# Another job beside the second pair's gates, and two casts on other engines, in the recurrent branch of a hybrid encoder

## The chip, the cores and the metric

The kernel runs on one core of a Trainium2 chip. The metric is device time in microseconds (us) of one execution. The engines work side by side, each through its own queue in a fixed order: TensorE (PE, matmuls), VectorE (DVE), ScalarE (ACT), GpSimd (POOL), and the SP queue, which issues all DMAs here. Matmuls write PSUM; DVE and ACT read PSUM and SBUF; the GpSimd work here is all in SBUF.

## The reference, cut to what matters

Two residual layers (1024 tokens, width 1024). The even layer projects its normed input once and feeds two branches, differential attention and a bidirectional gated linear recurrence (RG-LRU); the odd layer is a neighbourhood attention. The recurrent branch is what the change touches:

```python
xc = lax.conv_general_dilated(x, conv_w[:, None, :], ...) + conv_b      # depthwise, width 4
za = einsum('bsnc,rncd->rbsnd', xb, w_a) + b_a                         # r: two directions
zx = einsum('bsnc,rncd->rbsnd', xb, w_x) + b_x
gate_a, gate_x = sigmoid(za), sigmoid(zx)
log_a = -LRU_C * gate_a * softplus(-lam)
u = sqrt(-expm1(2.0 * log_a)) * gate_x * xc
h = forward scan of (a[0], u[0]) + backward scan of (a[1], u[1])
...
mixed = concatenate([a_out * silu(g_a), b_out * silu(g_b)])            # then @ w_out
```

The recurrence has 512 channels, which the kernel holds as four chunks of 128 partitions by 1024 tokens.

## The kernel before, in words

Matrix products are made from split operands: a high part (a cast to a reduced 32-bit type, `fp32r`) and a low part (the rest after subtraction), three matmuls per product (`mm3`, lines 201 to 203): high by high, high by low, low by high. So every activation or weight that enters a matmul needs a cast for its high part and a subtraction for its low part. For weights, `split_next` does it (L185 on ACT, `whi`; L186 on GpSimd, `wlo`), slab by slab in the order of `order0`, one slab per 128 output columns.

`proj` computes 128 output channels for one half of the tokens (512) with 24 matmuls and hands the PSUM bank to an evacuation. Four banks go around in the recurrent branch, two each of two kinds (`bank`); a bank is free again when its evacuation has read it.

The jobs of the branch, in program order (lines 851 to 855):

- `xb(c)`: projects chunk c of the recurrent input; evacuated by an ACT copy (L418).
- `cv(c)`, `conv(c)`: the convolution. For chunks 2 and 3 GpSimd makes the first tap (L705), DVE adds three (L710). Then comes the high part `xch` (L715 on ACT for chunks 0 and 1, L717 on DVE for 2 and 3) and the low part `xcl` in two halves (L720, on DVE for chunks 0 and 1, on GpSimd for 2 and 3).
- `pair((c, c+1))`: for two chunks, sixteen gate products of three matmuls (name `gate`), each with a sigmoid on ACT (L751), a tanh per direction (L757) and a product on DVE (L759); after the sixteen, for each direction an exponential (L766), squares (L770) with a DVE step (L771), square roots (L777), products (L780), scans (L783, L785) and their sum (L787). In between `gate_w` splits the gate weights of a later chunk (L730 on ACT, `gwh`; L731 on GpSimd, `gwl`).
- `vj(h)`: head h's values for the attention; evacuated by an ACT copy (L425).
- `gb(c)`: the branch's own gate path for chunk c. Each half is evacuated by a tanh on ACT (L667), a DVE step that reads PSUM for the last time (L668), a product with the scans' result (L795, DVE), a high part (L799, ACT), a low part (L800, DVE), both in a strided order, and two DMAs that store them (L802).
- `kq0` and one half of the next keys: what the attention starts with.

`weave` interleaves jobs by hand, so many steps of each in turn. The framework then fixes the order of each engine's instructions ahead of the run: it walks the program with its own estimates of when each instruction's inputs are there, and gives a free engine what is ready, by program order, evacuations and weight splits first (`high_priority`). On the chip each engine keeps that order, whatever is really ready.

## Time and profile before

| | us |
|---|---|
| runs | 1191.19, 1193.62, 1196.17 |
| median | 1193.62 |
| the profiled execution, own time | 1190.94 |
| its span | 1189.2 |
| granted TensorE clock, mean | 0.994 |

The span is from the first to the last instruction of the profiled execution. The recurrent branch with the jobs named above takes about 60 to 231 us of it; the attention's first logits follow at 230.75. In a timeline row the first number is the start and the second the length, both in us from the span's start; rows of several instructions are marked x2, x3. Brackets hold the idle time of the engine just before the row and what ended it.

### The profile page before, as it was taken

To read this page: it belongs to the slowest core of one execution; us is meant where nothing else is said; L and a number is where in the kernel's file an instruction comes from. 1 tells how busy PE (TensorE), PEld (TensorE's weight loads), DVE (VectorE), ACT (ScalarE), POOL (GpSimd) and SP (SyncE) were. 2 spreads that over 40 slices of the span, in tenths; PEclk is the share of its full clock that TensorE was granted. 3 is DMA by queue.
4 is the path that set the end of the run, shared out by engine and by line. 5 is a ranking of instruction groups with operands and counts; after the bars stand their busy time and mean duration, and the time that the engine had idled before them with its cause. 6 is when DMAs were issued, how large, how long until landed. Compare 5 with 4: busy or idle time off the path is not lost.

```text
span 1189.2 us, 19214 instructions
## 1 busy us (share of the span) xinstructions
PE 1142.0 (96%) x7232; PEld 972.3 (82%) x7232; DVE 735.6 (62%) x1422; ACT 564.4 (47%) x1029; POOL 372.5 (31%) x346
## 2 busy tenths in 40 slices
PE   4999899999998999999999999999999999999997
PEld 3788668888887888777878888988998998888896
DVE  6867948699889989768763334233434443556354
ACT  4358486465655556523443444344444434445121
POOL 2124321243333322344413333332333333326100
PEclk8999999999999999999999999999999999999999
DMA  9723132422123112476513442243453544314212
GB/s 331 234 87 117 53 96 74 141 74 82 37 79 88 32 39 72 136 245 225 181 53 121 136 116 83 87 141 101 131 171 96 152 133 120 90 38 161 92 72 71
DMA packets 85789, 136.46 MB, mean 115 GB/s; under 512 B 8000, under 2 KB 49472, under 8 KB 85696
## 3 DMA queue, kind: packets, MB, share of 16 engines
q1 hardware_dynamic: 85696, 135.23, 36.4%
q8 instruction: 57, 0.93, 0.3%
q14 instruction: 36, 0.29, 0.1%
HBM read 112.13 MB, written 16.78 MB: 108 GB/s over the span
## 4 chain that ended last, share of the span: by engine, by line
PE 75%; DVE 12%; ACT 5%; DMA 3%; issue 2%; POOL 2%; SPq 0%; DVEq 0%; ACTq 0%; POOLq 0%
PE pp L201 14%; PE pp L203 14%; PE pp L202 14%; PE no L1383 4%; PE etr L1365 3%; PE v L201 2%; PE v L203 2%; PE v L202 2%; PE n L662 2%; PE atr L998 2%; DVE e L968 2%; PE n L663 2%; PE s L662 1%; PE s L663 1%; POOL wlo L186 1%
## 5 line engine op out<-in xcount | busy, mean ns | idle before, releaser
L201 PE MATMUL pp<-ahi,whi 128*128 128x512 f32 (+1 forms) x976 | 370.2, 379 | 1.0 <-DVE sgb L668 0.9
L203 PE MATMUL pp<-ahi,wlo 128*128 128x512 f32 (+1 forms) x976 | 367.7, 377 | 1.1 <-POOL wlo L186 1.1
L202 PE MATMUL pp<-alo,whi 128*128 128x512 f32 (+1 forms) x976 | 368.0, 377 | 0.0
L186 POOL TENSOR_TENSOR wlo<-raw,whi 128x1024 fp32r<-128x1024 f32 x80 | 196.8, 2463 | 267.6 <-ACT whi L185 249.1
L203 PEld LDWEIGHTS pp<-ahi,wlo 128*128 128x128 f32 x976 | 183.8, 188 | 35.4 <-POOL wlo L186 1.6
L201 PEld LDWEIGHTS pp<-ahi,whi 128*128 128x128 f32 x976 | 183.8, 188 | 34.0 <-DVE sgb L668 1.7
L202 PEld LDWEIGHTS pp<-alo,whi 128*128 128x128 f32 x976 | 183.9, 188 | 30.4
L1354 POOL TENSOR_SCALAR e<-e,r 128x288 f32<-128x288 f32 (+1 forms) x128 | 71.5, 572 | 234.7 <-DVE r L1352 234.4
L185 ACT ACTIVATE whi<-raw 128x1024 fp32r<-128x1024 f32 x80 | 84.3, 1056 | 105.3 <-PE pp L202 57.4
L972 ACT ACTIVATE e<-e,nm 128x1024 f32<-128x1024 f32 x64 | 73.6, 1150 | 47.1 <-DVE nm L968 46.7
L1349 ACT ACTIVATE e<-e,nm 128x288 f32<-128x288 f32 (+1 forms) x128 | 72.7, 569 | 46.1 <-DVE nm L1346 39.3
L1371 DVE COPY e<-etr 96x384 f32<-96x384 f32 (+1 forms) x64 | 35.5, 555 | 94.3 <-PE etr L1365 92.7
L1346 DVE CUSTOM_DVE_ANT_0 e<-n,bias 128x288 f32<-128x288 f32 (+1 forms) x128 | 60.6, 505 | 46.9 <-PE n L663 32.9
L1369 ACT ACTIVATE e<-etr 96x384 f32<-96x384 f32 (+1 forms) x64 | 31.3, 490 | 118.2 <-DVE e L1371 116.7
L968 DVE CUSTOM_DVE_ANT_0 e<-s,tb 128x1024 f32<-128x1024 f32 x64 | 77.3, 1219 | 6.7 <-PE s L663 4.9
L989 POOL TENSOR_SCALAR e<-e,r 128x256 f32<-128x256 f32 x32 | 32.7, 1021 | 131.6 <-DVE r L978 81.4
L201 PE MATMUL v<-whi,ahi 128*128 128x256 f32 x256 | 72.2, 282 | 0.0
L203 PE MATMUL v<-whi,alo 128*128 128x256 f32 x256 | 71.9, 281 | 0.0
L202 PE MATMUL v<-wlo,ahi 128*128 128x256 f32 x256 | 71.9, 281 | 0.0
L1005 ACT ACTIVATE ath<-atr 128x512 fp32r<-128x512 f32 x64 | 37.5, 596 | 38.1 <-PE atr L998 37.8
L1365 PE MATMUL etr<-ident,e 128*96 128x128 f32 (+1 forms) x384 | 52.5, 272 | 2.0 <-POOL e L1354 2.0
L662 PE MATMUL s<-ks,qq 128*128 128x512 f32 x128 | 52.5, 410 | 0.4 <-DVE nm L968 0.4
(218 smaller groups left out, 2108.5 us busy)
## 6 DMA issues: line engine op xcount, KB each, us to landing
raw<-in_w_dram SPq DMA_DIRECT2D x56, 512.0 KB
ada<-in_adaw_dram SPq DMA_DIRECT2D x96, 256.0 KB
raw<-in_wo_dram SPq DMA_DIRECT2D x24, 512.0 KB
bias<-in_nab_dram SPq DMA_DIRECT2D x64, 144.0 KB
qq<-qq SPq DMA_DIRECT2D x48, 128.0 KB
bias<-in_nab_dram SPq DMA_DIRECT2D x32, 192.0 KB
xT<-in_xT_dram SPq DMA_DIRECT2D x16, 256.0 KB
vd<-vt SPq DMA_DIRECT2D x32, 128.0 KB
```

The costliest lines, as they stand in the source:

```text
L185: A.activation(hi[:], raw[:], AF.Copy)
L186: G.tensor_tensor(lo[:], raw[:], hi[:], ALU.subtract)
L201: T.matmul(ps, lh, rh, start=start, stop=False)
L202: T.matmul(ps, lh, rl, start=False, stop=False)
L203: state["pe"] = T.matmul(ps, ll, rh, start=False, stop=stop).ins
L662: T.matmul(dst, qsel(q[m]), k, start=True, stop=False)
L968: state["dve"] = V.tensor_tensor_reduce(out=e[:], in0=ps[:].rearrange("p a b -> p (a b)"), in1=tbt["tb"][:, o:o + S], scale=-1.0, scalar=3 ...
L972: A.activation(e[:], e[:], AF.Exp, scale=-1.0, bias=nm[:], accum_out=sums[:, m:m + 1])
L1346: state["dve"] = V.tensor_tensor_reduce(out=e[:, m, :n], in0=ps[:, m, :n], in1=bias["now"][m][:, :n], scale=-1.0, scalar=3.0e38, op0=ALU.a ...
L1349: A.activation(e[:, m, :n], e[:, m, :n], AF.Exp, scale=-1.0, bias=nm[:, m:m + 1], accum_out=sums[:, m:m + 1])
L1354: state["pool"] = G.tensor_scalar(e[:, m, :n], e[:, m, :n], r[:, m:m + 1], 0.0, ALU.mult, ALU.add).ins
L1365: T.transpose(pt[:kn, m, j * P:(j + 1) * P], e[:, m, j * kn:(j + 1) * kn], ident[:])
```

## The change

Three things:

1. `vj(3)` and `gb(1)` change places. The second pair's gates are woven with `vj(3)` (one step of it to two gates, as before with `gb(1)`), and `gb(1)` comes right after, ahead of `gb(2)`. The weight slabs change places with them.
2. The high part of the convolution is made on ACT for all four chunks; L717 on DVE goes.
3. For chunk 0 alone, `gb`'s high part (L799) is made by GpSimd.

```diff
-    order0 = [c_xb, c_xb + 1, c_v, c_xb + 2, c_xb + 3, c_v + 1, c_v + 2, c_gb, c_gb + 1]
-    order0 += [c_v + 3, c_gb + 2, c_gb + 3, c_k, c_q]
+    order0 = [c_xb, c_xb + 1, c_v, c_xb + 2, c_xb + 3, c_v + 1, c_v + 2, c_gb, c_v + 3]
+    order0 += [c_gb + 1, c_gb + 2, c_gb + 3, c_k, c_q]
...
             xl = [kqp.tile([P, HF], F32R, tag=t, name=f"xcl{c}", bufs=3) for t in ("qq1", "qlo")]
-            if c < 2:
-                A.activation(xh[:], xc[:], AF.Copy)
-            else:
-                V.tensor_copy(xh[:], xc[:])
+            A.activation(xh[:], xc[:], AF.Copy)
...
                 hi, lo = t[:].bitcast(F32R), lo[:].bitcast(F32R)
-                A.activation(as_fours(hi), by_fours(m), AF.Copy)
+                if c:
+                    A.activation(as_fours(hi), by_fours(m), AF.Copy)
+                else:
+
+                    G.tensor_copy(as_fours(hi), by_fours(m))
                 V.tensor_tensor(as_fours(lo), by_fours(m), as_fours(hi), ALU.subtract)
...
                 cv(2), cv(3), vj(1), vj(2), mod_step(), gb(0), mod_step(),
-                weave(gb(1), pair((2, 3)), turns=(1, 2)),
-                vj(3), gb(2), gb(3), kq0(), proj(at0[c_k + 1], 0, evac_k(("a", 1)))]
+                weave(vj(3), pair((2, 3)), turns=(1, 2)),
+                gb(1), gb(2), gb(3), kq0(), proj(at0[c_k + 1], 0, evac_k(("a", 1)))]
```

## The prediction

> **What bounds the kernel now.** I read the page first, then the windows of this branch, then what TensorE (PE) waits for, and last each engine's timeline around those waits.

> ```profile
> span 1189.2 us, 19214 instructions
> PE 1142.0 (96%) x7232; PEld 972.3 (82%) x7232; DVE 735.6 (62%) x1422; ACT 564.4 (47%) x1029; POOL 372.5 (31%) x346
> ```

> PE is busy for 96% of the span and its matmuls stay the same in number and shape. Only its idle time can go. The recurrent branch has this much of it, by the windows (stretch, its length, PE busy) and by the waits from 60 to 235 us (total, times, longest):

> ```profile
> 140.00:174.00 34.00, 27.43 (x113) 20.36 (x112) 20.33 (x21) 24.67 (x32) 13.24 (x11) 1.00 0.21 72
> ...
> 187.00:205.00 18.00, 18.00 (x81) 14.93 (x80) 17.06 (x11) 8.91 (x9) 2.68 (x1) 1.00 0.17 56
> ```

> ```profile
> PE gate L201 <- DVE sgb L668: 3.9, 2, 2.1
> PE gate L201 <- ACT t L751: 1.7, 1, 1.7
> PE pp L201 <- DVE sgb L668: 0.9, 1, 0.9
> PE gate L203 <- POOL gwl L731: 0.7, 1, 0.7
> PE gate L201 <- ACT gwh L730: 0.3, 1, 0.3
> ```

> From 140 to 174 us PE idles 34.00 - 27.43 = 6.57 us, which the waits explain (3.9 + 1.7 + 0.7 + 0.3 = 6.6). With the 0.9 later, 7.5 us is all the change can win here, 0.6% of the time. A difference of 0.5% (6.0 us) is about what a measurement of this kernel can tell from none. In 187 to 205 us PE is full while VectorE (DVE) is busy for 17.06 of 18: a chain on DVE runs just inside PE's cover there.

> The three large waits, on PE, then ScalarE (ACT), DVE and GpSimd (POOL); brackets hold the idle time before a row and its releaser:

> ```profile
> 143.35 0.50 PE L201 MATMUL gate<-xch,gwh 128*128 128x512 f32 x1 [1.85 <-DVE sgb L668]
> ...
> 147.77 0.50 PE L201 MATMUL gate<-xch,gwh 128*128 128x512 f32 x1 [2.05 <-DVE sgb L668]
> ...
> 151.31 0.50 PE L201 MATMUL gate<-xch,gwh 128*128 128x512 f32 x1 [1.66 <-ACT t L751]
> ```

> ```profile
> 133.56 0.60 ACT L667 ACTIVATE sgb<-pp 128x512 f32<-128x512 f32 x1 [3.28 <-PE pp L203]
> 144.42 1.15 ACT L799 ACTIVATE sgb<-t 128x512 fp32r<-128x512 f32 x1 [10.26 <-DVE t L795]
> ...
> 146.42 0.58 ACT L667 ACTIVATE sgb<-pp 128x512 f32<-128x512 f32 x1
> ...
> 148.31 1.27 ACT L751 ACTIVATE t<-gate,sm 128x512 f32<-128x512 f32 x2
> 149.60 1.08 ACT L799 ACTIVATE sgb<-t 128x512 fp32r<-128x512 f32 x1
> 150.58 0.67 ACT L751 ACTIVATE t<-gate,sm 128x512 f32<-128x512 f32 x1
> ```

> ```profile
> 140.91 0.66 DVE L717 CAST xch<-xc 128x1024 fp32r<-128x1024 f32 x1
> ...
> 142.63 0.67 DVE L668 SCALAR_TENSOR_TENSOR sgb<-sgb,pp 128x512 f32<-128x512 f32 x1
> 143.34 1.05 DVE L795 SCALAR_TENSOR_TENSOR t<-t,sgb 128x512 f32<-128x512 f32 x1
> 145.60 1.06 DVE L800 TENSOR_TENSOR ylo<-t,sgb 128x512 fp32r<-128x512 f32 x1 [1.22 <-ACT sgb L799]
> ...
> 147.03 0.69 DVE L668 SCALAR_TENSOR_TENSOR sgb<-sgb,pp 128x512 f32<-128x512 f32 x1 [0.23 <-ACT sgb L667]
> ```

> ```profile
> 141.70 3.85 POOL L720 TENSOR_TENSOR xcl<-xc,xch 128x512 fp32r<-128x512 f32 x2 [9.65 <-issue]
> ```

> PE's gates need PSUM banks. Two are held by gb(0)'s halves until L668. The first L668 comes at 142.63, behind the first pair's scans and the cast at 140.91. The second comes at 147.03: its tanh (146.42) is queued on ACT behind the high-part cast L799, which sat 10.26 us waiting for DVE. The third wait is for a sigmoid (150.58) behind the second L799 (149.60). So ACT's in-order wait feeds two of the three.

> **The change part by part.**

> *GpSimd takes gb(0)'s high part.* Two L799 leave ACT, and its 10.26 us wait with them: the second tanh and the sigmoids come soon after their matmuls. The third wait goes (-1.6 of 1.66; its sigmoid still takes 0.67). The second half's L668 stays in the queue behind the first half's L800, which now waits for GpSimd. The trace has no one-input GpSimd copy with these strides; the nearest row is the scaling

> ```profile
> L1354 POOL TENSOR_SCALAR e<-e,r 128x384 f32<-128x384 f32 x64 | 37.9, 605 | 148.3 <-DVE r L1352 147.9 <-PE n L663 0.3
> ```

> By size that is 605 x 512/384 = 0.8 us at the low end. The high end is one L720, 3.85/2 = 1.9 us. L800, a strided pass on DVE, takes 1.06 against 0.67 for L668, so I scale 0.8 by that to 1.25 us. That is no faster than L799's 1.15. [...] The second wait so keeps most of its length, 1.5 of 2.05, if the copy gets ahead of the second L720, and 1.9 more, 3.4, if it queues behind both. I take 1.5 (-0.55).

> *The convolutions' casts go to ACT.* For chunk 3, DVE's 0.66 at 140.91 leaves the queue ahead of L668, worth up to 0.66 on the first wait; ACT was idle there (the 10.26), so its cast costs nothing. I take -0.4, since GpSimd's L720 starts earlier and can hold up DVE. For chunk 2 it is another matter:

> ```profile
> 103.48 2.59 DVE L710 SCALAR_TENSOR_TENSOR xc<-xb,sm,xc 128x1023 f32<-128x1023 f32 x2
> 106.18 0.70 DVE L717 CAST xch<-xc 128x1024 fp32r<-128x1024 f32 x1
> 106.79 3.47 DVE L759 TENSOR_TENSOR t<-t,xc 128x1024 f32<-128x1024 f32 x2
> ```

> ```profile
> 101.44 0.69 ACT L751 ACTIVATE t<-gate,sm 128x512 f32<-128x512 f32 x1 [0.31 <-PE gate L203]
> ...
> 103.58 0.58 ACT L418 ACTIVATE xb<-pp 128x512 f32<-128x512 f32 x1
> 104.06 1.84 ACT L751 ACTIVATE t<-gate,sm 128x512 f32<-128x512 f32 x3
> ```

> ```profile
> 104.64 0.39 PE L201 MATMUL gate<-xch,gwh 128*128 128x512 f32 x1
> ```

> ```profile
> L715 ACT ACTIVATE xch<-xc x2: 1060/1061/1062, 74.1 to 78.7; 128x1024 fp32r<-128x1024 f32 x2
> ```

> L759 for chunk 1 was ready when the twelfth of the pair's sixteen sigmoids ended (101.44 + 0.69 = 102.13), and is written earlier in the program, yet DVE has the convolution and its cast ahead of it. So the plan that fixes each engine's order holds conv(2) for done before 102.13; on the chip it ends at 103.48 + 2.59 = 106.07. A cast on ACT would be placed by that same plan next to the twelfth sigmoid, ahead of the copy at 103.58 and the sigmoids at 104.06. ACT then waits until 106.07, casts for 1.06 (its other 128x1024 casts, the last row) until 107.13, makes the next weight's high part (a cast of that shape, 1.0), and copies xb (0.58) from 108.1 to 108.7. The bank of that copy is what the sixteenth gate at 104.64 writes next, by the order in which banks are handed out. PE stops from 104.64 to about 108.7: +4.05. If the cast lands ahead of the twelfth sigmoid it is +5.25; if it slips into a gap after its data, 0 to +0.4. I take 4.05. ACT's chain behind it moves as far as PE does, so the later waits keep their size. GpSimd's L720 for chunk 2 starts at 107.1, about as now, so the weights queued behind it are not later.

> *vj(3) is woven with the second pair.* vj(3) has the same 48 matmuls, and its evacuations are ACT copies of 0.58 alone. The gb(1) steps leave the weave:

> ```profile
> 157.82 1.13 ACT L799 ACTIVATE sgb<-t 128x512 fp32r<-128x512 f32 x1
> 158.83 0.64 ACT L730 ACTIVATE gwh<-gwr 128x512 fp32r<-128x512 f32 x1
> ```

> The last chunk's gate weights came 1.13 late behind that L799; the waits on gwh and gwl, 0.3 + 0.7, go (-1.0, bounds 0 and -1.0). Its four DMA stores on the SP queue move later with gb(1); the weight loads on that queue go by slab order, and two equal-sized slabs change places: 0.

> *gb(1) covers the second pair's tail.* Here is the bill:

> ```profile
> 187.76 1.23 DVE L780 TENSOR_TENSOR t<-t,w 128x1024 f32<-128x1024 f32 x1 [1.68 <-ACT w L777]
> 189.02 2.29 DVE L783 TENSOR_TENSOR_SCAN t<-t,t 128x1024 f32<-128x1024 f32 x1
> ...
> 194.32 4.49 DVE L785 TENSOR_TENSOR_SCAN w<-t,t 128x1024 f32<-128x1024 f32 x1
> ```

> ```profile
> 193.98 2.68 POOL L186 TENSOR_TENSOR wlo<-raw,whi 128x1024 fp32r<-128x1024 f32 x1 [8.40 <-ACT whi L185]
> ```

> ```profile
> 208.83 0.50 PE L201 MATMUL pp<-ahi,whi 128*128 128x512 f32 x1 [0.89 <-DVE sgb L668]
> ```

> DVE's chain starts at 187.76 when ACT's first square root is done, and it ends in the L668 that PE waits for at 208.83, with no slack (0.89). Ahead of that square root ACT gets two tanh (0.60) and two L799 (1.15) where it had one L799 and the vj(3) copies: 2 x 0.60 + 1.15 - 2 x 0.58 = +1.2. DVE gets 2 x (0.67 + 0.69 + 1.06) = 4.8 us more; before 187.76 it has room for that. I take +1.2, bounds 0 and 4.8 (all of it inside the chain).

> **The sum.** +4.05 - 1.6 - 0.55 - 0.4 - 1.0 + 1.2 = +1.7 us. The profiled execution took 1190.94 (span 1189.2); that gives 1192.6. The median of the runs is 1193.62, 2.7 above the profiled one; on that footing 1195.3. Its own range is 1191 to 1198.

> **The rivals.**

> *ScalarE does not wait at 102 us.* For it: ACT has idle gaps between sigmoids where a cast of 1.06 fits, if the plan puts it past 106. Against it: DVE's order above. Then 0.4 stands in place of 4.05: 1.7 - 3.65 = -1.95, 1191.7.

> *All waits go.* ACT does not wait, L668 of the second half gets ahead of L800, the tail costs nothing: -3.9 - 1.7 - 1.0 = -6.6, and half of the 0.9: -7, 1186.6. For it: nothing but order keeps L668 back, its tanh being ready early. Against it: the order now is L668, L795, L800, L668.

> *GpSimd and VectorE hold each other up.* The scan at 194.32 takes 4.49 where the one at 189.02 takes 2.29, and it ends 2.2 us after GpSimd's wlo (193.98 + 2.68 = 196.66): it stood still until GpSimd was done. If both L720 and the copies so alternate with L787, L795 and L800 from 140 us on, the second wait becomes 3.4 instead of 1.5 and the first gains nothing: 1.7 + 1.9 + 0.4 = +4.0, 1197.6. [...]

> *The tail decides (slower).* If gb(1)'s DVE work lands inside the chain from 187.76 on, PE waits there 4.8 in place of 1.2, and if the sixteenth gate loses 5.25: 1.7 + 3.6 + 1.2 = +6.5, 1200.1. It decides once the second half's L800 starts after the pair's first L780. For it: the chain's 17.06 of 18. Against it: gb(1) is the first job after the last gate, and DVE still idles (1.68 before 187.76) when the chain starts.

> **How the numbers follow.** Chances: forecast 0.38, no wait on ScalarE 0.20, all waits go 0.18, mutual hold-up 0.12, the tail 0.12. Faster by over 0.5% (below 1187.7) is the third, with a little of the second: 0.20. Slower (above 1199.6) is the last: 0.13 with a little of the fourth. Within: 0.67. The range runs from 1186 (the third) to 1199.5, leaving out the tail and what lies below.

> **What would show it.** Right: on ACT a cast L715 near 102 us idle for 4 us on DVE's L710; a gate on PE idle for about 4 us near 104; no L799 before 151; a GpSimd copy of about 1.25 us; no wait on gwl; a longer wait than 0.9 near 210. Wrong: an L715 past 106 with no wait before it, or a second L668 ahead of the first L800.

## The result, and the profile after

| | us |
|---|---|
| before, median of 6 runs | 1193.57 |
| after, median of 6 runs | 1206.88 (1204.86 to 1211.76) |
| after over before | 1.0114, 95% interval 1.0092 to 1.0136 |
| predicted | 1195.3, range 1186 to 1199.5 |
| profiled execution after, its span, its mean clock | 1208.87, 1207.2, 0.983 |

The kernel became 13.3 us slower, and the upper end of the prediction's range lies 7.4 us below it. The page of the changed kernel says at once that no work was added:

```profile
span 1207.2 us, 19218 instructions
...
PE 1153.3 (96%) x7232; PEld 980.5 (81%) x7232; DVE 736.2 (61%) x1420; ACT 565.0 (47%) x1029; POOL 373.9 (31%) x348
```

TensorE has the same 7232 matmuls and yet 11.3 us more busy time (1153.3 against 1142.0). Longer waits can't do that: matmuls of unchanged shape took longer. The windows of the branch show where (stretch, length, busy time of PE, its weight loads, DVE, ACT and POOL, then the granted clock; the last two columns are DMA):

```profile
104.00:114.00 10.00, 4.51 (x12) 3.26 (x11) 6.06 (x5) 4.44 (x6) 4.51 (x3) 0.66 0.00 0
140.00:174.00 34.00, 26.98 (x106) 20.88 (x106) 22.85 (x17) 14.18 (x19) 13.04 (x10) 0.90 0.18 62
159.00:165.00 6.00, 5.64 (x13) 4.51 (x14) 2.32 (x4) 2.42 (x3) 1.09 (x1) 0.50 0.63 218
...
208.00:231.00 23.00, 20.70 (x85) 16.61 (x84) 20.52 (x16) 8.38 (x10) 4.20 (x2) 0.93 0.31 107
```

Before, the clock column was 1.00 from 60 to 231 us. Now it is 0.66, 0.50 and 0.93 in three places, and each place begins with a wait. On TensorE's timeline:

```profile
104.16 0.39 PE L201 MATMUL gate<-xch,gwh 128*128 128x512 f32 x1
110.04 0.79 PE L201 MATMUL gate<-xch,gwh 128*128 128x512 f32 x1 [5.49 <-ACT t L748]
110.63 0.63 PE L202 MATMUL gate<-xcl,gwh 128*128 128x512 f32 x1
111.06 0.63 PE L203 MATMUL gate<-xch,gwl 128*128 128x512 f32 x1
...
153.18 0.50 PE L201 MATMUL gate<-xch,gwh 128*128 128x512 f32 x1 [2.50 <-DVE sgb L668]
...
159.35 0.80 PE L201 MATMUL gate<-xch,gwh 128*128 128x512 f32 x1 [3.85 <-DVE sgb L668]
...
164.64 0.63 PE L201 MATMUL gate<-xch,gwh 128*128 128x512 f32 x1
165.07 0.45 PE L202 MATMUL gate<-xcl,gwh 128*128 128x512 f32 x1
...
221.91 0.50 PE L201 MATMUL pp<-ahi,whi 128*128 128x512 f32 x1 [2.30 <-DVE sgb L668]
```

Read the starts, not the lengths: 110.63 to 111.06 is 0.43 us from one matmul to the next, where the usual step is 0.227 (20 steps from 214.69 to 219.22 us). Each slow matmul costs 0.2 us. There are 8 after the first wait, 13 after the third (159.35 to 164.64), 8 after the last one.

With that the branch adds up. From the first gate matmul to the attention's first logit it took 153.03 us before and 166.19 after, 13.16 more, about the 13.3 by which the medians differ. (The two profiled executions differ by 17.9; some 1.5 of the rest lie in the start, some 3 behind 640 us, and the changed kernel's runs scatter by 6.9.) Its waits of 0.25 us or more sum to 7.46 before and 14.82 after: +7.36. The 29 slow matmuls add 29 x 0.2 = 5.8. Sum: 13.16. What is left, 145.57 us, is the same in both.

The two new causes of waiting. On ScalarE and VectorE, the chunk-2 cast (L714 here) stands ahead of the twelfth sigmoid:

```profile
101.55 1.14 ACT L754 ACTIVATE w<-t,a 128x1024 f32<-128x1024 f32 x1
108.36 1.06 ACT L714 ACTIVATE xch<-xc 128x1024 fp32r<-128x1024 f32 x1 [5.67 <-DVE xc L710]
109.32 0.67 ACT L748 ACTIVATE t<-gate,sm 128x512 f32<-128x512 f32 x1
```

```profile
105.67 2.59 DVE L710 SCALAR_TENSOR_TENSOR xc<-xb,sm,xc 128x1023 f32<-128x1023 f32 x2
...
150.39 2.14 DVE L784 TENSOR_TENSOR t<-t,w 128x1024 f32<-128x1024 f32 x1
152.45 0.67 DVE L668 SCALAR_TENSOR_TENSOR sgb<-sgb,pp 128x512 f32<-128x512 f32 x1
153.16 1.06 DVE L792 SCALAR_TENSOR_TENSOR t<-t,sgb 128x512 f32<-128x512 f32 x1
155.48 3.09 DVE L801 TENSOR_TENSOR ylo<-t,sgb 128x512 fp32r<-128x512 f32 x1 [1.26 <-POOL sgb L800]
...
158.63 0.67 DVE L668 SCALAR_TENSOR_TENSOR sgb<-sgb,pp 128x512 f32<-128x512 f32 x1
```

The convolution ends at 105.67 + 2.59 = 108.26; ScalarE stood idle for it since the tanh. And on GpSimd, with the weight's low part (L186) between the two copies:

```profile
149.39 4.29 POOL L717 TENSOR_TENSOR xcl<-xc,xch 128x512 fp32r<-128x512 f32 x2 [7.97 <-ACT xch L714]
...
154.34 1.10 POOL L800 CAST sgb<-t 128x512 fp32r<-128x512 f32 x1
155.41 2.35 POOL L186 TENSOR_TENSOR wlo<-raw,whi 128x1024 fp32r<-128x1024 f32 x1
160.09 1.09 POOL L800 CAST sgb<-t 128x512 fp32r<-128x512 f32 x1 [2.34 <-DVE t L792]
```

VectorE's subtraction L801 has its operands at 155.4 but ends at 158.57, some 0.8 us after GpSimd's L186 (157.76); it took 3.09 where it took 1.06 before. The L668 that TensorE waits for is queued behind it. The copy itself was not late: VectorE idled 1.26 us for it, where it had idled 1.22 us for ScalarE's cast before.

### The profile page after: what moved, and what is told of

It reads as the page before. It is cut to its first block, busy times and chain, and to the rows that moved or that the text cites. A ratio compares the mean times of both kernels' runs of the same rounds, so it can differ in the third digit from the quotient of the medians.

```text
span 1207.2 us, 19218 instructions
## 1 busy us (share of the span) xinstructions
PE 1153.3 (96%) x7232; PEld 980.5 (81%) x7232; DVE 736.2 (61%) x1420; ACT 565.0 (47%) x1029; POOL 373.9 (31%) x348
## 4 chain that ended last, share of the span: by engine, by line
PE 72%; DVE 14%; ACT 5%; DMA 4%; POOL 2%; issue 2%; SPq 0%; DVEq 0%; ACTq 0%; POOLq 0%
PE pp L201 14%; PE pp L203 14%; PE pp L202 14%; PE no L1384 4%; PE etr L1366 3%; PE v L201 2%; PE v L202 2%; PE v L203 2%; PE n L662 2%; PE atr L999 2%; DMA ada<-in_adaw_dram 2%; DVE e L969 2%; PE n L663 2%; PE s L662 1%; PE s L663 1%
## 5 line engine op out<-in xcount | busy, mean ns | idle before, releaser
L201 PE MATMUL pp<-ahi,whi 128*128 128x512 f32 (+1 forms) x976 | 371.6, 381 | 2.4 <-DVE sgb L668 2.3
L203 PE MATMUL pp<-ahi,wlo 128*128 128x512 f32 (+1 forms) x976 | 368.8, 378 | 1.1 <-POOL wlo L186 1.1
L186 POOL TENSOR_TENSOR wlo<-raw,whi 128x1024 fp32r<-128x1024 f32 x80 | 196.9, 2463 | 281.1 <-ACT whi L185 252.8
L201 PEld LDWEIGHTS pp<-ahi,whi 128*128 128x128 f32 x976 | 184.7, 189 | 35.6 <-DVE sgb L668 2.7
L203 PEld LDWEIGHTS pp<-ahi,wlo 128*128 128x128 f32 x976 | 184.4, 189 | 35.7 <-POOL wlo L186 1.6
L185 ACT ACTIVATE whi<-raw 128x1024 fp32r<-128x1024 f32 x80 | 84.3, 1056 | 106.0 <-PE pp L202 57.4
L201 PE MATMUL v<-whi,ahi 128*128 128x256 f32 x256 | 73.1, 286 | 0.0
L203 PE MATMUL v<-whi,alo 128*128 128x256 f32 x256 | 72.7, 284 | 0.0
```

Source lines behind the costliest of these rows:

```text
L185: A.activation(hi[:], raw[:], AF.Copy)
L186: G.tensor_tensor(lo[:], raw[:], hi[:], ALU.subtract)
L201: T.matmul(ps, lh, rh, start=start, stop=False)
L203: state["pe"] = T.matmul(ps, ll, rh, start=False, stop=stop).ins
```

## The experiments

All times are medians, ratios are to the kernel before with a 95% interval. The kernel before was timed anew with each group of experiments (medians 1192.68 us for e1 to e4, 1192.27 for e5 to e8, 1194.03 for e9 to e11), so kernels of different groups are compared by their ratios. "Branch" is first gate matmul to first logit in the profiled execution. "Slow matmuls" are those of the branch at half rate in that one execution; another execution of the same kernel can have more or fewer (the last section shows why).

| kernel | us | ratio | branch | waits | slow matmuls |
|---|---|---|---|---|---|
| before | 1193.57 | | 153.03 | 7.46 | 0 |
| after | 1206.88 | 1.0114 [1.0092, 1.0136] | 166.19 | 14.82 | 29 |
| e1_c2_on_dve | 1197.20 | 1.0039 [1.0023, 1.0054] | 156.95 | 9.18 | 13 |
| e2_casts_only | 1202.42 | 1.0085 [1.0069, 1.0101] | 163.08 | 12.67 | 21 |
| e3_weave_only | 1195.89 | 1.0025 [1.0015, 1.0035] | 153.73 | 5.86 | 12 |
| e4_gpsimd_only | 1196.85 | 1.0046 [1.0028, 1.0063] | 156.19 | 8.31 | 12 |
| e5_cast_behind_sigmoid | 1202.00 | 1.0070 [1.0050, 1.0091] | 159.82 | 10.92 | 19 |
| e6_copies_together | 1195.06 | 1.0020 [1.0006, 1.0034] | 154.12 | 7.19 | 7 |
| e7_fill_the_wait | 1211.21 | 1.0160 [1.0136, 1.0183] | 169.81 | 14.10 | 31 |
| e8_late_split | 1189.09 | 0.9971 [0.9959, 0.9984] | 149.52 | 4.42 | 0 |
| e9_fill_ahead | 1203.86 | 1.0091 [1.0076, 1.0106] | 162.81 | 9.37 | 19 |
| e10_both_mended | 1193.59 | 1.0004 [0.9990, 1.0018] | 153.96 | 7.53 | 7 |
| e11_weave_and_chunk3 | 1194.91 | 1.0014 [1.0000, 1.0027] | 156.68 | 9.15 | 10 |

Branch less waits less 0.2 per slow matmul is 145.0 to 146.2 us in every row (in e7 and e9 after 4.1 us of added matmuls is taken off too). So within about 1.2 us the branch is TensorE's work plus its waits plus its slow matmuls.

**e1_c2_on_dve**: the changed kernel, chunk 2 cast on VectorE again.

```diff
-            A.activation(xh[:], xc[:], AF.Copy)
+            if c == 2:
+                V.tensor_copy(xh[:], xc[:])
+            else:
+                A.activation(xh[:], xc[:], AF.Copy)
```

> The changed kernel, with chunk 2's high part back on VectorE (chunk 3's stays on ScalarE). Theory A (the cast queued on ScalarE ahead of its data stops TensorE for 5.5 us near 104 and its clock is at half for about 4 us after, some 2 us more): 7 to 8 of the 13.3 us lost come back, so 5 to 6.5 us slower than before; what is left sits at gb(0) and in the tail. Theory B (the loss is GpSimd at gb(0), whose copies and weight split hold VectorE): nothing or under 2 us comes back. Theory C (the tail, gb(1) behind the second pair): the same as B.

The wait near 104 us and its slow matmuls are gone, and the ratio falls from 1.0114 to 1.0039: this one cast costs about 0.75%, 9 us. The branch says the same, 166.19 - 156.95 = 9.2 us.

**e2_casts_only**: the kernel before with both casts on ScalarE.

```diff
-            if c < 2:
-                A.activation(xh[:], xc[:], AF.Copy)
-            else:
-                V.tensor_copy(xh[:], xc[:])
+            A.activation(xh[:], xc[:], AF.Copy)
```

> The kernel before with only the casts moved to ScalarE. Theory A: 7 to 8 us slower than before, with a wait of about 5.5 us on a gate near 104 and slow matmuls behind it, nothing new later. Theories B and C: within 2 us of before.

Without the other parts of the change the two casts cost 0.85%: a wait of 4.93 us for the sigmoid behind the cast, with 9 slow matmuls behind it. The second pair's waits are 2.50, 2.04 and 0.96, against 1.85, 2.05 and 1.66 before, but 12 matmuls are slow there too.

**e3_weave_only**: the kernel before with `vj(3)` and `gb(1)` exchanged, in `order0` and in the jobs.

```diff
-                weave(gb(1), pair((2, 3)), turns=(1, 2)),
-                vj(3), gb(2), gb(3), kq0(), proj(at0[c_k + 1], 0, evac_k(("a", 1)))]
+                weave(vj(3), pair((2, 3)), turns=(1, 2)),
+                gb(1), gb(2), gb(3), kq0(), proj(at0[c_k + 1], 0, evac_k(("a", 1)))]
...
```

> The kernel before with only vj(3) and gb(1) changing places. Theory A: no wait near 104; the waits on the gate weights (1.0) do not go, since they are in the changed kernel too (0.7 left), and the tail's wait grows from 0.9 to 2.3 with slow matmuls behind it: 1 to 3 us slower. Theory C: 5 us or more slower. Theory B: within 2 us.

The waits fall from 7.46 to 5.86, yet the branch is 0.7 longer and the ratio 1.0025. The tail's wait grows to 2.32, as expected, but the slow matmuls come elsewhere. On its TensorE timeline:

```profile
145.62 0.50 PE L201 MATMUL gate<-xch,gwh 128*128 128x512 f32 x1 [1.86 <-DVE sgb L668]
...
146.69 0.63 PE L202 MATMUL pp<-alo,whi 128*128 128x512 f32 x1
...
150.03 0.80 PE L201 MATMUL gate<-xch,gwh 128*128 128x512 f32 x1 [1.00 <-DVE sgb L668]
```

In this execution matmuls turn slow 1.1 us behind a wait of 1.86, 12 of them, while before ran its 1.85, 2.05 and 1.66 without one; the last section shows what the difference hangs on.

**e4_gpsimd_only**: the kernel before with GpSimd's copies for chunk 0.

```diff
-                A.activation(as_fours(hi), by_fours(m), AF.Copy)
+                if c:
+                    A.activation(as_fours(hi), by_fours(m), AF.Copy)
+                else:
+                    G.tensor_copy(as_fours(hi), by_fours(m))
```

> The kernel before with only gb(0)'s high part on GpSimd. Theory A: the two waits for L668 stay, the one for the sigmoid goes: 0 to 2 us faster. Theory B: the second wait for L668 grows from 2.05 to about 3.9 and the clock halves behind it: 3 to 5 us slower. Theory C: no change.

Slower by 0.46%, as theory B has it, if a little more. GpSimd, then VectorE:

```profile
143.03 3.84 POOL L720 TENSOR_TENSOR xcl<-xc,xch 128x512 fp32r<-128x512 f32 x2 [9.65 <-issue]
...
147.51 1.06 POOL L802 CAST sgb<-t 128x512 fp32r<-128x512 f32 x1
148.53 2.34 POOL L186 TENSOR_TENSOR wlo<-raw,whi 128x1024 fp32r<-128x1024 f32 x1
```

```profile
148.60 3.08 DVE L803 TENSOR_TENSOR ylo<-t,sgb 128x512 fp32r<-128x512 f32 x1 [2.89 <-POOL sgb L802]
...
151.75 0.67 DVE L668 SCALAR_TENSOR_TENSOR sgb<-sgb,pp 128x512 f32<-128x512 f32 x1
```

The copy is queued behind both halves of the convolution's low part (2.89 idle on VectorE), and the weight's low part then holds the subtraction up. The second wait becomes 4.55 instead of 2.05. ScalarE is relieved, and its sigmoid is no longer waited for, but that was the smaller bill.

**e5_cast_behind_sigmoid**: the changed kernel, the chunk-2 cast still on ScalarE but queued behind the first pair's last sigmoid.

```diff
-            A.activation(xh[:], xc[:], AF.Copy)
+            with tc.issue_after(state["sig"]) if c == 2 else nullcontext():
+                A.activation(xh[:], xc[:], AF.Copy)
...
```

> The changed kernel with one edit: ScalarE still casts chunk 2, but the cast is queued behind the first pair's last sigmoid instead of ahead of the 12th. Theory A (the place in ScalarE's queue): the 5.5 us wait near 110 us and its half-clock matmuls go, and the time is that of the kernel with chunk 2 back on VectorE, about 1197 us (1195 to 1200). Theory B (ScalarE has too much to do, wherever the cast stands): the cast's 1.06 us and its wait stay in the way, and the time stays within 3 us of the changed kernel's 1206.9.

Neither came true. The wait near 110 is gone, as the theory of the queue's place has it, but the time is 1202.0, not 1197. The cast now starts at 121.15, and the order on VectorE comes out differently at the second pair:

```profile
144.61 0.66 DVE L668 SCALAR_TENSOR_TENSOR sgb<-sgb,pp 128x512 f32<-128x512 f32 x1
145.19 1.66 DVE L786 TENSOR_TENSOR t<-t,w 128x1024 f32<-128x1024 f32 x1
146.77 1.79 DVE L794 SCALAR_TENSOR_TENSOR t<-t,sgb 128x512 f32<-128x512 f32 x1
149.76 3.08 DVE L803 TENSOR_TENSOR ylo<-t,sgb 128x512 fp32r<-128x512 f32 x1 [1.21 <-POOL sgb L802]
```

A sum of scans (L786) now stands between L668 and its product L794, and the product takes 1.79 beside GpSimd (1.07 in e1). GpSimd's first copy starts at 148.68, when the product (148.56) and GpSimd's own work ahead of it (148.59) are both done, and the second wait is 5.96 us against 3.86 in e1, with 12 slow matmuls against 6. Branch against e1: +1.74 of waits and 6 x 0.2, together the 2.9 measured. The ratios differ by 0.31%, 3.7 us, and their intervals overlap, so the timings don't contradict that sum.

**e6_copies_together**: e4, with the weight's low part queued behind the second copy.

```diff
-            G.tensor_tensor(lo[:], raw[:], hi[:], ALU.subtract)
+            with tc.issue_after(state["copy"]) if i == at0[c_gb] + 2 else nullcontext():
+                G.tensor_tensor(lo[:], raw[:], hi[:], ALU.subtract)
...
```

> The kernel before with GpSimd's two copies for the first gate block, but the low part of the weight that GpSimd makes between them (2.34 us) queued behind the second copy. Theory A (VectorE's subtraction is held up by that weight split, and the second gate's matmuls with it): the subtraction goes from 3.08 back to about 1.06 us, the wait before the second evacuation from 4.55 to about 2.2 us, and the time from 1196.9 to 1193 to 1195 us. Theory B (what costs is only that the copies stand behind GpSimd's convolution work): the second wait stays above 4 us and the time above 1196.

The subtraction ahead of the second L668 (L669 here) is back at its old length:

```profile
149.20 1.03 DVE L804 TENSOR_TENSOR ylo<-t,sgb 128x512 fp32r<-128x512 f32 x1 [2.89 <-POOL sgb L803]
```

The second wait is 3.40, and the branch 2.1 us shorter than in e4. The time, 1195.06, lies 0.06 above the band expected, and the intervals of the two ratios overlap. The hold-up by the weight's low part is shown by the row; the 2.89 of idle that is left is the place behind both convolution halves, so both theories hold a part.

**e7_fill_the_wait**: the changed kernel with 18 matmuls more, whose result nobody reads, meant for the wait near 104 us.

```diff
+                            fill = c == 1 and r == 1 and g == 0 and hf == 1
+                            if fill:
+                                junk = ptp.tile([P, HF], F32, tag="pt", name="junk")
+                                with tc.issue_after(state["pe"]):
+                                    for n in range(18):
+                                        last = T.matmul(junk[:], wh[:, i, :], xh[:, cs],
+                                                        start=n == 0, stop=n == 17)
...
```

> The changed kernel with 18 matmuls more, of 128x512, whose result nobody reads, put into TensorE's 5.5 us wait near 105 us. Theory A (TensorE's clock is halved after idle time): the 8 to 9 matmuls behind the wait run at 0.227 instead of 0.427 us from start to start, and the time is 1 to 2 us below the changed kernel's although there is more work. Theory B (the slow matmuls have another cause, such as the operands just written by ScalarE and VectorE): they stay slow, and the time stays the same or grows by up to 1 us.

It missed its place by one gate:

```profile
109.10 0.79 PE L201 MATMUL gate<-xch,gwh 128*128 128x512 f32 x1 [5.82 <-ACT t L756]
109.69 0.63 PE L202 MATMUL gate<-xcl,gwh 128*128 128x512 f32 x1
110.11 0.63 PE L203 MATMUL gate<-xch,gwl 128*128 128x512 f32 x1
110.54 5.27 PE L752 MATMUL junk<-xch,gwh 128*128 128x512 f32 x18
```

The fillers ran behind the wait, so they don't test whether filling it helps. They do speak on theory B: the first five start 0.427 us apart and the others 0.227, though all 18 read the same two operands. And the 18 x 0.227 = 4.1 us of matmuls outside a wait made the branch 3.6 us longer and the median 4.3.

**e9_fill_ahead**: the same with `hf == 0`, one gate earlier.

> The changed kernel with the same 18 matmuls more as in e7_fill_the_wait, now queued one gate earlier, ahead of the gate that waits. Theory A (the clock is halved because TensorE stood idle): 4.1 of the 5.5 us are filled, the wait that is left is 1 to 2 us, the gates behind it go at 0.227 us from start to start, and the time is 1 to 2 us below the changed kernel's 1206.9 although it has 4.1 us more work. Theory B (the slow matmuls come from what else runs at that place): they stay slow behind the shorter wait, and the time stays at 1206 to 1208.

```profile
105.17 4.24 PE L752 MATMUL junk<-xch,gwh 128*128 128x512 f32 x18
109.75 0.50 PE L201 MATMUL gate<-xch,gwh 128*128 128x512 f32 x1 [0.34 <-ACT t L756]
110.09 0.39 PE L202 MATMUL gate<-xcl,gwh 128*128 128x512 f32 x1
110.32 0.40 PE L203 MATMUL gate<-xch,gwl 128*128 128x512 f32 x1
```

ScalarE's cast is as late as ever, TensorE waits 0.34 instead of 5.49, and the same gates go at 0.23 from start to start. With 4.1 us more work the kernel is 3.0 us faster than the changed one (ratios 1.0091 and 1.0114; their intervals overlap a little, but the branch is 3.4 shorter). The cast, the sigmoids and the convolution still run there, so the slow matmuls at this place come from TensorE's idling and not from them.

**e10_both_mended**: the changed kernel with the edits of e1 and e6 together.

> The changed kernel with chunk 2 cast on VectorE and the weight's low part queued behind GpSimd's second copy, so with both of the mends that single edits pointed to. Theory A (the two costs are separate and add): the time of e1_c2_on_dve less the 1.8 us that the second mend gave alone, about 1195.4 us (1194 to 1197). Theory B (the mends overlap, since both shorten the same waits of the second pair): no gain over e1_c2_on_dve, 1197 to 1198.5.

1.0004: the loss is gone, and 1.8 us below what was expected. The subtraction ahead of the second L668 takes 1.03 us and the second wait is 1.79, against 3.09 and 3.86 in e1. In ratios, the loss of 1.14% is 0.75% for the chunk-2 cast (after to e1), 0.35% for the weight's low part between the copies (e1 to e10), and 0.04% for the rest, which is within the interval and can hide gains against losses.

**e11_weave_and_chunk3**: the edit of e1, and all copies on ScalarE.

> The changed kernel with chunk 2 cast on VectorE and the first gate block's copies on ScalarE: what is left is the new weave and the chunk-3 cast on ScalarE. Theory A (GpSimd's copies cost the same here as alone, 3 to 4 us): 1193 to 1194.5 us. Theory B (what is left over beyond before is the weave's, with its later tail): 1195.5 to 1197, as the weave alone gave 1195.9.

1194.91 lies between the two. Against e1 the GpSimd copies as they stood cost 0.25%, with intervals that overlap a little. Against e10 (1.0004) the intervals overlap too: whether well-placed GpSimd copies are better than ScalarE's stays open.

**e8_late_split**: the kernel before with only chunk 3's cast on ScalarE, and the high and low parts and stores of `gb(0)` put off: woven in as a job of their own, each queued behind the latest sigmoid.

```diff
-                weave(gb(1), pair((2, 3)), turns=(1, 2)),
+                weave(gb(1), pair((2, 3)), late_split(), turns=(1, 2, 1)),
...
+        def late_split():
+            yield 0.0
+            for args in stash:
+                with tc.issue_after(state["sig"]):
+                    split_gb(*args)
+                yield 0.0
```

> The kernel before with two other edits: ScalarE casts chunk 3 alone, and the first gate block's high and low parts and their stores are queued behind the second pair's last sigmoid, so that neither ScalarE's cast nor VectorE's subtraction stands ahead of the next evacuation. Theory A (the waits at the start of the second pair come from what is queued ahead of evacuations and sigmoids): the waits of 2.05 and 1.66 us go, and the time is 2 to 4 us below before, 1189 to 1191 us. Theory B (these waits are bound by the data itself, or the deferred work holds the first stores up): no change, 1192 to 1195 us.

Faster than both kernels: 1189.09, ratio 0.9971. Its waits from 60 to 260 us:

```profile
PE gate L201 <- DVE sgb L668: 2.3, 1, 2.3
PE gate L203 <- POOL gwl L731: 1.2, 2, 0.7
PE pp L201 <- DVE sgb L668: 0.9, 1, 0.9
```

The waits of 2.05 and 1.66 are gone, 3.0 us less waiting in all, and no matmul of the branch is slow. ScalarE and VectorE do the same work as before but for one cast; only its place in their queues differs. The two edits weren't run apart. That the late split made the gain is read from the waits: the one that chunk 3's cast bears on, the first, is longer than before (2.30 against 1.85).

## Why the prediction was wrong, step by step

Two steps failed. The sum had no term for matmuls at half clock behind a wait, which took 5.8 us. And its waits were 5.7 us short, most of all the second wait, where it left out the weight's low part that GpSimd makes between the two copies.

- *Chunk 2's cast on ScalarE, +4.05.* The mechanism held: a cast queued ahead of its data by a plan that thinks the convolution done. It landed ahead of the twelfth sigmoid, the case priced at +5.25, and the wait was 5.49. The size failed for what no step of the sum had: 8 slow matmuls behind it, 1.6 us. Taken out (e1), it was worth 9.2 us of the branch: those 7.1, and another 8 slow matmuls later on, 0.2 of the first wait and 0.4 in the rest. Whether those later ones are the cast's doing or chance isn't shown.
- *Third wait gone, -1.6.* Right: no wait for a sigmoid is left in the second pair.
- *Second wait, -0.55.* Wrong, and the wait that was most misjudged: +1.80 (3.85), and 13 slow matmuls, 2.6 us. The copy itself was well sized, 1.10 us where I took 1.25 between 0.8 and 1.9. Its place behind both halves of L717, priced at 3.4 and not taken, is where it came, and that cost nothing here: GpSimd was done with what stood ahead at 154.25 and the copy's input was written at 154.22. (In e4, where VectorE casts chunk 3, that place cost VectorE 2.89 us of idle time.) What failed is that I costed the copy and not its neighbour behind it: the weight's low part came next and stretched L801 by 2.0. With that part moved away (e10 against e1) the second wait is 1.79 instead of 3.86.
- *First wait, -0.4.* It grew by 0.65. With the cast gone from VectorE, the sum of scans (L784) comes beside GpSimd's L717 and takes 2.14 instead of 1.21, so that VectorE needs 4.37 us from the start of its scan to L668 where it needed 3.92; that is 0.45 of the 0.65. Among the kernels that cast chunk 3 on ScalarE, e1, e8, e10 and e11 wait 2.3 us here and e2 2.5. It isn't so in all: e5, where the sum comes behind L668, waits 1.73, and e7 and e9, where the sum takes as long, 1.9 to 2.0. The rest of the growth stays open.
- *Gate weights, -1.0.* -0.33: the wait on `gwh` went, the 0.68 on `gwl` stayed. The bound "0" was nearer.
- *Tail, +1.2.* +1.41 in the wait (2.30 against 0.89), as worked out: from the last gate matmul to ScalarE's first square root it takes 18.8 us in every kernel with the new weave and 17.4 to 17.5 in every one with the old, and from there to the end of the wait 22.1 to 22.2 in all. The 8 slow matmuls that came with it, 1.6 us, were in no term.

The waits thus moved by +7.36 where the sum had +1.7, and the clock added 5.8. Of the rivals, mutual hold-up was right in kind: for the first wait it named the right pair (the sum of scans and GpSimd's L720), for the second the right subtraction on VectorE, but not the weight's low part beside it. The tail did not decide. The range was too narrow on the slow side because each wait was priced at its length. The trace of before held the warning, but outside this branch: six slow matmuls from 529 us on, behind a wait of 1.70. That its waits in the branch had none behind them was luck, as the last section shows.

## What to carry to other kernels

An operation moved to a less busy engine has to be placed in that engine's queue, not only afforded by its idle time: what it waits for is then waited for by everything behind it (here ScalarE idled 5.67 us ahead of the chunk-2 cast, and TensorE 5.49 us for the sigmoid behind it), and what stands beside it there can hold up another engine (GpSimd's L186 of 2.35 us, beside which VectorE's subtraction took 3.09 instead of 1.06). Price a wait on TensorE by its length plus some 7 to 13 matmuls at half rate behind it (1.4 to 2.6 us here), as a risk, even where the trace of before shows none in that stage. By the figures of the next section, as an estimate, a single wait under 1.6 us carries no such risk, one of 3.9 us or more carries it always (one of its halves of 1.93 falls into one step), and in between it depends on where the edges of the steps fall.

## What the runs showed of the hardware

```profile
219.77:223.19 3.42, 1.28 (x6) 1.06 (x7) 3.39 (x4) 1.24 (x2) 2.11 (x1) 1.00 0.21 77
223.19:226.60 3.41, 3.41 (x10) 2.63 (x9) 2.23 (x3) 1.60 (x2) 0.31 (x1) 0.50 0.16 62
...
208.03:211.45 3.42, 1.50 (x7) 0.92 (x5) 3.42 (x4) 2.88 (x4) 0.43 (x1) 1.00 0.36 137
211.45:214.86 3.41, 3.01 (x13) 2.51 (x14) 2.51 (x2) 0.83 (x1) 1.99 (x1) 1.00 0.04 16
```

- In the profiled execution of before, the edges cut the waits of 1.85, 2.05 and 1.66 so that no step held more than 1.60 us of idle time; in e3 the wait of 1.86 fell whole into one step.
- A VectorE subtraction of 128x512 took 3.08 to 3.21 us beside a GpSimd subtraction of 2.34 to 2.41, and 1.03 to 1.08 without one (after, e4, e6, e10): it ended only some 0.8 to 0.9 us after GpSimd's had.
- GpSimd's copy of 128x512 in a strided order took 1.05 to 1.12 us, no longer than ScalarE's 1.08 to 1.15 for the same block (before, e2, e8).
